# One planner for the output projection and the memory attention: the second half of a transformer layer issued by the list of streams that already issues its first half

## The chip, the cores and the metric

The kernel runs on one core of a Trainium2 chip. A core has TensorE (PE, matrix products into PSUM), VectorE (DVE), ScalarE (ACT), GpSimd (POOL) and SyncE (SP), which here issues all transfers. Each engine takes its instructions strictly in the order in which the program gives them, and waits at an instruction until the semaphores it names have been raised; the engines run beside one another. The metric is the time of one execution on the device in microseconds, as the median of several runs. The kernel before took 1528.05 us (1527.91 to 1530.81 in 3 runs).

## What is computed

One layer of an encoder on 1024 tokens of 1024 features, all in float32. Of the reference, cut to what matters here:

```
h = rmsnorm(x, g_mix_pre);  proj = h @ w_in
y_fox = forgetting_attention(...)            # 8 heads, causal
y_chk = chunked_relpos_attention(...)        # 8 heads, banded
y = concat(rmsnorm(y_fox, g_fox_out), rmsnorm(y_chk, g_chk_out))
x = x + rmsnorm(y @ w_out, g_mix_post)       # output projection
h = rmsnorm(x, g_mem_pre); mem_n = rmsnorm(mem, g_mem_kv)
q = h @ w_mq; k = mem_n @ w_mk; v = mem_n @ w_mv      # 4 heads of 256, 256 memory tokens
y = softmax(q k^T / 16) v @ w_mo
x = x + rmsnorm(y, g_mem_post)
h = rmsnorm(x, g_ff_pre)
x = x + rmsnorm(square(relu(h @ w_ff1)) @ w_ff2, g_ff_post)
```

## The kernel before

**Arithmetic.** Each float32 operand is split in two parts of the type float32r, high (a copy by ACT) and low (the difference, by DVE or POOL). A product is three matmuls, high by high, high by low and low by high (`mm3`, L189 to L193). A weight block of 128 x 1024 is loaded into one of three buffers `wraw`, split by ACT into `whi` and by DVE into `wlo` (two buffers each), and used.

**Tokens.** The tokens are worked in two halves of 512, `th` 0 and 1, and in rows of 128 (`b`). Output features are in two halves `nh`. PSUM has eight banks in four pairs, `mm`, `s`, `tr` and `pv`; a pair is what lets PE write one bank while the other is read.

**The planner.** The attention of both head groups is issued by a small planner that runs while the program is built: class `Flow` (L56). Work is written as streams, generators whose steps each have a cost in PE time and a condition; `Flow.run` (L106) takes, again and again, the first stream in the list whose next step is ready, and what PE's steps bring for the other engines goes to lists with a due time (`put`, L70; `upto`, L86). `Tokens` (L39) count free buffers, `seen` holds when a result is there. `Stock` (L351) holds one list of weight blocks that it loads and splits as buffers come free (`pump`, L401). In the kernel before, its list ends with the memory's key and value weights, `w_mk` and `w_mv`; `memory_steps` (L824), the last filler of the attention phase (L874), makes memory keys `km` and values `vm` with them. All of `w_mk` and `w_mv` has its low part made by DVE, in two halves.

**After attention.** What follows is plain code (L951 to L1150), whose order within each engine a general scheduler of the language decides when the program is built:

- `head_outputs` (L957) loads the stored head outputs of one token half and one group `g` back (`oin`), makes the parts of `yT` and the sums of squares `sq`; `head_rstd` (L981) turns them into a factor for each row by a small matmul `ssh`.
- `mix_out` (L1000) is the output projection, PE tile `yw`: eight blocks of 12 matmuls for each (th, g). With g = 0 ACT evicts a block into `yw` (L1022), with g = 1 DVE adds it (L1024), ACT takes the sum of squares (L992) and DVE multiplies by the gain (L1026). `w_out` is loaded in 12 blocks: those of g = 0 serve both halves, those of g = 1 are loaded for each half.
- `close_block` (L1046) ends four rows: two small POOL operations for a reciprocal root (L200, L201), the residual add (L1053), a store of the row, a sum of squares, a root again, and the normalised row (L1058). `turn` (L1060) transposes the rows on PE (`tr_h`) into `h2T` or `h3T` (L229, L230).
- `cross` (L1064) is the memory attention of one token half: for each head two query blocks `mq`, parts `qh`, `ql` (L1076, L1077), scores `ms`, softmax, transposes `mtr`, and the context product `mo`, into `oT`.
- `mem_out` (L1030) is the output product with `w_mo`, PE tile `ym`. For the second half of tokens `nh` 0 comes from `mem_out`, and `nh` 1 from a list written out by hand from L1363 on, which also issues the last row norms, the transposes `trx` and the first products of the feed-forward part. That hand-written part follows without a planner until the end of the kernel.

Of the kernel before, what the change touches and what calls it, by code (L numbers as in the profile page):

```python
# [55 lines left out]
class Flow:  # L56
# [77 lines left out]
def build(ctx, tc, nc, out, t):  # L134
# [182 lines left out]
    def values(g, w, vs, kb):  # L317
# [8 lines left out]
        if g == 0:  # L326
# [8 lines left out]
            dict(s=2, tr=2, pv=2, mm=2, sp=1, p=2, klo=4, bias=2, raw=2, w=0, u4=6).items()}  # L335
# [15 lines left out]
    class Stock:  # L351
# [3 lines left out]
        def __init__(self):  # L355
            self.blocks = []
            for n, (kind, pr) in enumerate(ORDER):
# [4 lines left out]
                if n > 3:  # L362
                    self.blocks.append((("v", n), t["w_v"][n - 4], [P, KC, P]))
                self.blocks.append((("k", n), t["w_qk"][b + 4], [P, KC, P]))
            self.blocks.append("mem")
            self.blocks += [(("mk", nb), t["w_mk"][nb], [P, KC, P]) for nb in range(KC)]
            self.blocks += [(("mv", nh, kp), row_pair(t["w_mv"], kp, nh), [P, 2, HT])
                            for nh in range(2) for kp in range(4)]
            self.raw, self.w, self.turned = {}, {}, 0
# [10 lines left out]
        def hi(self, key):  # L380
            raw, nm = self.raw[key], "_".join(map(str, key))
            w = [wp.tile(list(raw.shape), F32R, tag=x, bufs=2, name=x + nm) for x in ("whi", "wlo")]
# [3 lines left out]
        def lo(self, key, eng, half):  # L386
            raw, (hi, lo) = self.raw[key], self.w[key]
            n = raw.shape[1] // 2
# [3 lines left out]
        def split_now(self, n):  # L392
# [6 lines left out]
            seen.update({("raw", key): 0.0 for key in self.to_split})  # L399

        def pump(self):  # L401
# [16 lines left out]
            while self.to_split and free["w"].ready() and there(("raw", self.to_split[0])):  # L418
                free["w"].take()
                key = self.to_split.pop(0)  # L420
                vec = key[0] in ("mk", "mv")
                self.turned += 1

                def halves(at, key=key, eng="V" if vec else "G"):
                    cost = 0.61 if eng == "V" else 1.3
                    e = nc.vector if eng == "V" else nc.gpsimd
                    last = lambda end: (seen.__setitem__(key, end), free["raw"].give(end))
                    flow.put(eng, at, cost, lambda: self.lo(key, e, 0), lambda end: flow.put(
                        eng, end, cost, lambda: self.lo(key, e, 1), last, 2), 2)
# [82 lines left out]
    def score_steps():  # L512
        for n, a in heads:
# [57 lines left out]
            for what, m in (("u4", 2), ("klo", 1)):  # L571
                for _ in range(m):
                    free[what].give(flow.end)

# [51 lines left out]
    def value_steps():  # L626
        for n, a, g in units:
# [23 lines left out]
            def leave(pv=pv, nm=f"{n}{a}{g}", own=own, oth=oth, kcol=kcol, g=g, step=1 if kind == "f" else -1):  # L651
# [6 lines left out]
                        ot[own].rearrange("p a b -> p (a b)"))))))  # L658
# [7 lines left out]
    def all_of(key, m):  # L666
# [3 lines left out]
        def one(at):  # L670
            count[0] -= 1
            count[1] = max(count[1], at)
            if count[0] == 0:
                seen[key] = count[1]
        return one
# [148 lines left out]
    def memory_steps(keep):  # L824
        km = Act("km", NM)
        for nb in range(KC):
            for kc in range(0, KC, 2):
                yield 0.72, lambda: kc and there(("mT", kc)) or there(("mk", nb), ("mT", 0)) and free["mm"].ready()
# [7 lines left out]
            free["w"].give(flow.end)  # L836
# [3 lines left out]
        vh = [u4(f"vm_hi{m}", (P, D)) for m in range(2)]  # L840
        vl = [u4(f"vm_lo{m}", (P, D)) for m in range(2)]
        for nh, bank in enumerate(("mm", "s")):
            cs = slice(nh * HT, (nh + 1) * HT)
            ps = []
            for kp in range(4):
                for m in range(2):
                    yield 1.362, lambda: there(("mv", nh, kp)) and (kp or m or free[bank].ready(2))
# [8 lines left out]
                    if kp == 3:  # L856
                        flow.put("S", flow.end, 0.6, lambda m=m, p=ps[m], cs=cs: nc.scalar.activation(vh[m][:, cs], p, AF.Copy),
                                 lambda at, m=m, p=ps[m], cs=cs: flow.put("V", at, 0.7, lambda: nc.vector.tensor_sub(
                                     vl[m][:, cs], p, f(vh[m][:, cs])), free[bank].give, 1), 1)
                free["w"].give(flow.end)  # L860
        keep += [km, vh, vl]

# [11 lines left out]
    def attention_phase():  # L874
# [6 lines left out]
        flow.pumps += [stock.pump, biases.pump]  # L881
        flow.run([value_steps(), turn_steps(), score_steps(), side_steps(), filler_steps(keep)])
        return keep

    flip = [0]
    quiet = [False]

    def lo_eng():
        flip[0] ^= 1
        return nc.vector if flip[0] or quiet[0] else nc.gpsimd  # L890

    def row_pair(w, kp, nh):
        return w[kp * 2 * P:(kp + 1) * 2 * P, nh * HT:(nh + 1) * HT].rearrange(
            "(a p) n -> p a n", p=P)
# [56 lines left out]
    quiet[0] = True  # L951
# [4 lines left out]

    def head_outputs(th, g):  # L957

        yh = [u4(f"yT_hi{th}{g}{i}", (P, 2, HT)) for i in range(2)]
        yl = [u4(f"yT_lo{th}{g}{i}", (P, 2, HT)) for i in range(2)]  # L960
        sq = u4(f"sq{th}{g}", (P, HT), F32)
        for i in range(2):
            o = u4(f"oin{th}{g}{i}", (P, 2, HT), F32)
            for j in range(2):
                kc = g * 4 + i * 2 + j
                nc.sync.dma_start(o[:, j, :], od[kc][th])
                gc = gcol[:, kc:kc + 1]
                dh = yh[i][:, j, :]
                nc.scalar.activation(dh, o[:, j, :], AF.Copy, scale=gc)
                nc.vector.scalar_tensor_tensor(yl[i][:, j, :], o[:, j, :], gc, f(dh),  # L970
                                               op0=ALU.mult, op1=ALU.subtract)
            if i == 0:
                nc.scalar.activation(sq, o[:, 0, :], AF.Square)
                nc.scalar.activation(o[:, 1, :], o[:, 1, :], AF.Square)
            else:
# [832 lines left out]
```

## Time and profile before

| what | value |
|---|---|
| median of 3 runs | 1528.05 us |
| the profiled execution | 1528.19 us |
| its span, first to last instruction | 1526.4 us |
| granted TensorE clock, mean | 0.995 |
| busy: PE, DVE, ACT, POOL | 98%, 62%, 52%, 23% of the span |

The span is what the profiler sees; 1.8 us of the execution lie around it. Times in the views count from the start of the span. The stretch that the change touches runs from the last heads of attention (from about 470 us) to the first transposes of the feed-forward part (`trx`, first at 900.4 us). A matmul's record lasts longer than the distance from its start to the next one's, since matmuls are pipelined; so a PE that is "busy" all the time is not always at its full rate, and the granted clock and the distance between starts have to be read beside it. In the views of waits a line reads: who waited, for whom, total us, times, longest us. In the view of stages each row gives a stretch and its length, then the busy time and the count for PE, PE's weight loads, DVE, ACT and POOL, then the granted clock, the mean share of the 16 transfer engines and GB/s.

### The profile page before, as it was taken

How to read it: one execution, taken by the hardware profiler on the slowest of the kernel's cores; microseconds unless marked ns; L12 is line 12 of the kernel's file. 1: busy time of each engine (PE TensorE's matmuls, PEld its weight loads, DVE VectorE, ACT ScalarE, POOL GpSimd, SP SyncE). 2: the span in 40 equal slices, each digit the busy share in tenths (PEclk: the TensorE clock that was granted, in tenths of full speed). 3: DMA queues.
4: the chain of work that ended last, by engine and by line, in shares of the span. 5: the costliest groups of instructions: out<-in, count | busy, mean ns of one | idle time of the engine just before them, and what ended most of it. 6: DMA issues, size and time to landing. Idle time of an engine off the chain costs nothing. (4 is left out here: it accounts for less than half of the span.)

```text
span 1526.4 us, 21650 instructions
## 1 busy us (share of the span) xinstructions
PE 1492.2 (98%) x7692; PEld 1258.5 (82%) x7692; DVE 945.1 (62%) x1656; ACT 793.1 (52%) x1405; POOL 358.3 (23%) x558
## 2 busy tenths in 40 slices
PE   8999999999999999989999999999999999999998
PEld 7989888788888977778888787888888878888886
DVE  6477676565566755875465477665555575746577
ACT  5367676565566656444344445554555543444442
POOL 4244343343242200221020321433233000000021
PEclk9999999999999999999999999999999999999999
DMA  4222221413123453551252155674445595435575
GB/s 167 88 82 79 80 69 63 147 53 85 38 79 107 143 197 125 178 194 56 70 185 64 43 206 198 223 265 156 152 152 177 199 368 195 150 125 196 190 248 193
DMA packets 83854, 220.68 MB, mean 145 GB/s; under 512 B 9865, under 2 KB 13969, under 8 KB 83746
## 3 DMA queue, kind: packets, MB, share of 16 engines
q1 hardware_dynamic: 83746, 219.30, 43.2%
q8 instruction: 61, 1.00, 0.3%
q14 instruction: 47, 0.39, 0.1%
HBM read 159.96 MB, written 50.91 MB: 138 GB/s over the span
## 5 line engine op out<-in xcount | busy, mean ns | idle before, releaser
L617 DVE TENSOR_TENSOR pl<-ptr,ph 128x512 fp32r<-128x512 f32 (+1 forms) x152 | 91.7, 616 | 43.8 <-ACT ph L620 35.8
L620 ACT ACTIVATE ph<-ptr 128x512 fp32r<-128x512 f32 (+1 forms) x152 | 78.9, 540 | 56.4 <-PE ptr L611 51.1
L1534 ACT ACTIVATE whif<-ra 128x1024 fp32r<-128x1024 f32 x37 | 39.2, 1060 | 121.2 <-PE fy L192 62.6
L1536 DVE TENSOR_TENSOR wlof<-ra,whif 128x1024 fp32r<-128x1024 f32 x37 | 45.3, 1224 | 91.5 <-ACT whif L1534 91.5
L1650 POOL TENSOR_SCALAR rf<-sf 128x1 f32<-128x1 f32 x8 | 8.2, 1027 | 326.9 <-ACT jf L1635 326.6
L186 DVE TENSOR_TENSOR wlo<-wraw,whi 128x1024 fp32r<-128x1024 f32 x44 | 53.6, 1222 | 48.6 <-ACT whi L185 48.3
L647 PE MATMUL pv<-ph,vs 128*128 128x256 f32 x304 | 80.0, 287 | 0.0
L648 PE MATMUL pv<-pl,vs 128*128 128x256 f32 x304 | 78.8, 283 | 0.3 <-DVE pl L617 0.3
L185 ACT ACTIVATE whi<-wraw 128x1024 fp32r<-128x1024 f32 x44 | 46.3, 1058 | 50.0 <-PE ym L193 19.0
L192 PE MATMUL fx<-vlof,whif 128*128 128x512 f32 x168 | 65.5, 390 | 0.0
L193 PE MATMUL fx<-vhif,wlof 128*128 128x512 f32 x168 | 65.4, 389 | 0.0
L191 PE MATMUL fx<-vhif,whif 128*128 128x512 f32 x168 | 65.4, 389 | 0.0
L648 PEld LDWEIGHTS pv<-pl,vs 128*128 128x128 f32 x304 | 57.6, 189 | 5.1 <-DVE pl L617 0.8
L647 PEld LDWEIGHTS pv<-ph,vs 128*128 128x128 f32 x304 | 57.3, 189 | 3.8
L1424 POOL TENSOR_TENSOR sc<-wf,wf 128x512 f32<-128x512 f32 x14 | 22.1, 1581 | 143.6 <-DMA wf<-in_w_ff 111.7
L191 PE MATMUL yw<-whi,yT_hi 128*128 128x512 f32 x128 | 50.4, 400 | 5.2 <-ACT yw L1022 2.8
L191 PE MATMUL k<-hT_hi,whik 128*128 128x512 f32 x128 | 52.8, 412 | 0.0
L191 PE MATMUL mq<-h2T_hi,whi 128*128 128x512 f32 x128 | 51.7, 405 | 0.8 <-DVE yw L1024 0.8
L192 PE MATMUL ym<-wlo,oT_hi 128*128 128x512 f32 x128 | 50.9, 398 | 1.0 <-DVE wlo L186 1.0
L192 PE MATMUL mq<-h2T_lo,whi 128*128 128x512 f32 x128 | 51.6, 403 | 0.0
L193 PE MATMUL mq<-h2T_hi,wlo 128*128 128x512 f32 x128 | 51.5, 402 | 0.0
L191 PE MATMUL q<-hT_hi,whiq 128*128 128x512 f32 x128 | 50.8, 397 | 0.0
(605 smaller groups left out, 5026.2 us busy)
## 6 DMA issues: line engine op xcount, KB each, us to landing
ra<-gd SPq DMA_DIRECT2D x56, 512.0 KB, 3.9
wg<-in_w_ff SPq DMA_DIRECT2D x56, 512.0 KB, 5.2
wf<-in_w_ff SPq DMA_DIRECT2D x38, 512.0 KB, 3.8
gd<-s SPq DMA_DIRECT2D x48, 256.0 KB, 2.1
wraw<-in_w_mq SPq DMA_DIRECT2D x16, 512.0 KB, 4.4
wraw<-in_w_mo SPq DMA_DIRECT2D x16, 512.0 KB, 3.8
gd<-u SPq DMA_DIRECT2D x32, 256.0 KB, 2.1
gd<-g SPq DMA_DIRECT2D x25, 256.0 KB, 2.4
```

The costliest lines, as they stand in the source:

```text
L185: nc.scalar.activation(hi, raw, AF.Copy)
L186: (lo_on or nc.gpsimd).tensor_sub(lo, raw, f(hi))
L191: nc.tensor.matmul(ps, lh, rh, start=start, stop=False, skip_group_check=more)
L192: nc.tensor.matmul(ps, lh, rl, start=False, stop=False, skip_group_check=more)
L193: nc.tensor.matmul(ps, ll, rh, start=False, stop=stop, skip_group_check=more)
L617: flow.put("V", at, 0.7, lambda: nc.vector.tensor_sub(pl[:, live, :], tr[:, live, :], f(ph[:, live, :])), done)
L620: flow.put("S", flow.end, 0.6, lambda ph=ph, tr=tr, live=live: nc.scalar.activation(ph[:, live, :], tr[:, live, :], AF.Copy), split)
L647: nc.tensor.matmul(pv, v, ph[:, hs, :], start=c == 0 and half == 0, stop=False)
L648: nc.tensor.matmul(pv, v, pl[:, hs, :], start=False, stop=c + 1 == len(steps) and half == 1)
L1424: eng.tensor_sub(sc[:, k1], r0[:, k0], r1[:, k0])
L1534: nc.scalar.activation(ah, ra, AF.Copy)
L1536: nc.vector.tensor_sub(al, ra, f(ah))
```

## The change

The plain code between the attention and the hand-written list is replaced by streams of the same planner. `Flow.run` is called a second time, with the list

```
[memory_out_steps(), memory_turn_steps(), memory_score_steps(), rstd_steps(1), second_rows(), second_filler()]
```

so that, whenever its condition holds, a context product, a transpose of probabilities, a score or a transpose of rows is issued, and otherwise the next step of the filler, which is: output projection for g = 0 and for g = 1, queries of half 0, product with `w_mo` of half 0, queries of half 1, and the product of half 1 for `nh` 0. Of the rest:

- All weight blocks, `w_out`, `w_mq` and `w_mo` too, are in the one list of `Stock`. `w_out` is loaded in 8 blocks, and the projection with g = 1 no longer loads its blocks twice. A block's parts live in one of three homes: the `whi`/`wlo` pair, a further pair `wq`, or the general tiles `u4`. DVE makes a low part in one pass instead of two halves; four of the eight `w_mk` blocks have theirs made by POOL in two halves.
- Within the projection the order of the loops changes: one token half is done for both `nh` before the other.
- `Outputs` loads the head outputs of g = 0 as soon as the last scores are issued, in the attention phase; `rstd_steps(0)` is one of the streams there. Its last squares are taken in passes of 512 instead of 1024.
- `Rows` loads the residual rows, two at a time; `close_row` replaces `close_block` by a chain for each row, which begins when its last block is evicted. The two halves of a sum of squares are now added by the POOL operation that adds the constant, and 12 small DVE reductions fall away.
- The loads of the memory tokens stand one place earlier in the list of weights, before the last key block of attention.
- The last four `w_mo` blocks (half 1, `nh` 1) are loaded and split by `Stock` instead of after `mem_out`. The hand-written list itself is not changed.

The diff, cut to its core:

```diff
-    def run(self, streams):
+    def run(self, streams, more=lambda: False):
...
-        while any(h[1] for h in heads):
+        while any(h[1] for h in heads) or more():
...
+        last = self.now
         self.upto(math.inf)
+        self.now = last
...
+            self.blocks += [(("wo", g, nh, i), row_pair(t["w_out"], 2 * g + i, nh), pair)
+                            for g in range(2) for nh in range(2) for i in range(2)]
+            for th in range(2):
+                self.blocks += [(("mq", th, h, nb), t["w_mq"][h * 2 + nb], [P, KC, P])
+                                for h in range(4) for nb in range(2)]
+                self.blocks += [(("mo", th, nh, kp), row_pair(t["w_mo"], kp, nh), pair)
+                                for nh in range(2) for kp in range(4)]
+            self.home = {("wo", 0, 1, 0): "wq", ("wo", 0, 1, 1): "u4", ("wo", 1, 1, 0): "wq", ("wo", 1, 1, 1): "u4"}
+            self.home.update({("mk", nb): "u4" for nb in range(1, KC, 2)})
+            self.home.update({("mv", nh, kp): "u4" for nh in range(2) for kp in (1, 3)})
...
-                vec = key[0] in ("mk", "mv")
+                vec = key[0] not in "qkv" and (key[0] != "mk" or key[1] % 2)
...
+    def mix_steps(g):
+        for th, nh in ((0, 0), (0, 1), (1, 0), (1, 1)):
+            cs = slice(nh * HT, (nh + 1) * HT)
+            for b in range(4):
+                c = slice(b * P, (b + 1) * P)
+                for k in range(4):
+                    yield (0.681, lambda: k % 2 or there(("wo", g, nh, k // 2)) and (k or
+                           there(("y", th, g), ("rs", th, g)) and free["mm"].ready()
+                           and (("w", th) in ys or free["u4"].ready(4))))
...
+    def second_filler():
+        yield from mix_steps(0)
+        yield from mix_steps(1)
+        yield from query_steps(0)
+        yield from product_steps(0, (0, 1))
+        yield from query_steps(1)
+        yield from product_steps(1, (0,))
...
-        flow.run([value_steps(), turn_steps(), score_steps(), side_steps(), filler_steps(keep)])
+        flow.pumps += [stock.pump, biases.pump, outputs.pump]
+        flow.run([value_steps(), turn_steps(), score_steps(), side_steps(), rstd_steps(0),
+                  filler_steps(keep)])
...
-    mix_out((0,), 1)
-    mixed(0)
-    mix_out((1,), 1, after={1: turn_mixed(0)})
-    mixed(1)
...
-    o = cross(1, h2[1], after={0: lambda: turn(y0, 0, h3[0], "h3")})
+    with tc.manual_schedule():
+        free["wq"].give(flow.now)
+        for key, src in (("mix", "g_mix_post"), ("mem", "g_mem_pre")):
+            gains[key] = gain(p2, t[src], src)
+        flow.pumps[1] = Rows().pump
+        flow.run([memory_out_steps(), memory_turn_steps(), memory_score_steps(), rstd_steps(1), second_rows(),
+                  second_filler()], lambda: stock.to_load or stock.to_split)
...
-    mem_out(1, o, y, ss, gmpost, (0,))
-    wo = [load_w(row_pair(t["w_mo"], kp, 1), [P, 2, HT], u4, lo_eng()) for kp in range(4)]
+    wo = [stock.w["mo", 1, 1, kp] for kp in range(4)]
```

More of the change, by code (lines that the diff above doesn't have):

```diff
@@ L399, in split_now, with done @@
             seen.update({("raw", key): 0.0 for key in self.to_split})
+        def done(self, key):
+            home = self.home.get(key, "w")
+            for _ in range(1 + (home == "u4")):
+                free[home].give(flow.end)
         def pump(self):
@@ L626, in value_steps @@
     def value_steps():
+        landed = [all_of(("od", k), 32) for k in range(2)]
         for n, a, g in units:
@@ new lines, in build, with rstd_steps, add, root @@
+    outputs = Outputs()
+    def rstd_steps(g):
+        for th in range(2):
+            yield 0.5, lambda: there(("sq", th, g)) and free["pv"].ready()
+            free["pv"].take()
+            sq = parts[th, g][2]
+            rs = parts["rs", th, g] = small.tile([P, 4], F32, tag="rs4", bufs=4, name=f"rs{th}{g}")
+            ps = mm_tile([P, 4], f"ssh{th}{g}", "pv")
+            for b in range(4):
+                nc.tensor.matmul(ps[:, b:b + 1], sq[:, b * P:(b + 1) * P], o512, start=True, stop=True)
+            free["u4"].give(flow.end)
+            def add(rs=rs, ps=ps):
+                nc.vector.tensor_scalar(rs, ps, EPS, None, op0=ALU.add)
+            def root(at, rs=rs, key=("rs", th, g)):
+                free["pv"].give(at)
+                flow.put("G", at, 1.1, lambda: nc.gpsimd.tensor_tensor(rs, rs, mhalf[:, 0:4], op=ALU.pow), mark(key))
+            flow.put("V", flow.end, 0.16, add, root)
@@ L955, in build @@
     p2x = pool("p2x", stack=p2xs)
[L957 to L975, printed above, removed]
-                nc.scalar.activation(o, o, AF.Square)
-                nc.vector.tensor_add(sq, sq, o[:, 0, :])
-            nc.vector.tensor_add(sq, sq, o[:, 1, :])
-        return yh, yl, sq
```

549 lines of the change are left out of this document (362 added, 187 removed).

## The prediction

> **What bounds the kernel now.** I read the page first: the span, the shares of the engines and the chain that ended last.
>
> ```profile
> span 1526.4 us, 21650 instructions
> PE 1492.2 (98%) x7692; PEld 1258.5 (82%) x7692; DVE 945.1 (62%) x1656; ACT 793.1 (52%) x1405; POOL 358.3 (23%) x558
> PE 38%; DVE 1%; ACT 0%; DMA 0%; issue 0%; DVEq 0%; POOLq 0%; SPq 0%; POOL 0%; ACTq 0%
> ```
>
> TensorE (PE) is the bound and everything else runs beside it. The built programs hold 7740 matmuls each, in the same shapes, so the change can only move the time in which PE stands still or runs slowly. The next view cuts the changed stretch (515 to 885 us) by stages; columns are PE, weight loads, DVE, ACT, POOL, granted clock, DMA share and GB/s.
>
> ```profile
> 515.00:548.00 33.00, 31.57 (x171) 26.55 (x170) 21.07 (x36) 18.15 (x28) 1.77 (x7) 1.00 0.77 255
> 548.00:600.00 52.00, 48.69 (x222) 38.89 (x220) 23.25 (x34) 30.45 (x45) 3.06 (x3) 1.00 0.33 105
> 600.00:650.00 50.00, 47.57 (x216) 38.24 (x216) 38.42 (x50) 22.76 (x43) 9.87 (x17) 1.00 0.56 179
> 650.00:680.00 30.00, 25.37 (x106) 19.78 (x105) 21.99 (x32) 14.76 (x31) 8.24 (x16) 0.89 0.57 193
> 680.00:780.00 100.00, 100.00 (x511) 84.50 (x511) 48.94 (x85) 41.91 (x88) 8.43 (x18) 1.00 0.25 80
> 780.00:870.00 90.00, 90.00 (x473) 76.48 (x472) 50.05 (x85) 41.55 (x84) 23.20 (x37) 1.00 0.33 106
> 870.00:885.00 15.00, 12.84 (x48) 9.64 (x47) 8.39 (x9) 8.19 (x14) 2.17 (x2) 0.89 0.36 129
> 919.00:937.00 18.00, 14.77 (x70) 11.43 (x68) 16.10 (x25) 10.10 (x17) 0.00 (x0) 1.00 0.31 108
> 1250.00:1300.00 50.00, 50.00 (x222) 41.39 (x221) 25.18 (x23) 20.14 (x22) 0.00 (x0) 1.00 0.62 219
> ```
>
> PE idles 1.43 + 3.31 + 2.43 + 4.63 + 2.16 = 13.96 us between 515 and 885; the cross attention itself (680 to 870) has no idle at all. The view of waits, cut to 535 to 885, names what it waits for:
>
> ```profile
> PE yw L191 <- ACT yw L1022: 2.8, 3, 1.3
> PE ms L193 <- DVE ql L1077: 2.4, 1, 2.4
> PE yw L191 <- DVE yw L1024: 2.4, 3, 1.1
> PE mv L192 <- DVE wlomv L390: 1.3, 2, 1.1
> PE tr_h L216 <- DVE h2T_lo L230: 1.1, 2, 0.7
> PE ym L191 <- ACT whi L185: 1.1, 1, 1.1
> PE ym L192 <- DVE wlo L186: 1.0, 2, 0.8
> PE mq L191 <- DVE yw L1024: 0.8, 1, 0.8
> ```
>
> Each is PE standing at the head of its fixed order for an eviction, a row norm or a weight split while other matmuls could have run. The longest, and what follows it, in order of time:
>
> ```profile
> 667.81 0.28 PE L192 MATMUL ms<-km_lo,qh 128*128 128x256 f32 x1
> 670.51 0.39 PE L193 MATMUL ms<-km_hi,ql 128*128 128x256 f32 x1 [2.42 <-DVE ql L1077]
> ...
> 671.34 0.40 PE L191 MATMUL mq<-h2T_hi,whi 128*128 128x512 f32 x1
> 671.57 0.41 PE L192 MATMUL mq<-h2T_lo,whi 128*128 128x512 f32 x1
> ...
> 672.20 0.63 PE L191 MATMUL mq<-h2T_hi,whi 128*128 128x512 f32 x1
> 672.63 0.63 PE L192 MATMUL mq<-h2T_lo,whi 128*128 128x512 f32 x1
> ```
>
> A matmul of 512 columns starts 0.23 us after the one before (50 / 222 in the dense window); after the stall it takes 0.43, and so for some 3 us. The granted clock of 0.89 in two windows says what this costs: 0.11 x 30 + 0.11 x 15 = 4.95 us. A record lasts 0.39 where starts lie 0.23 apart, so each of the 15 waits listed also loses about 0.16 us of overlap that idle time does not show: 2.4 us. What can be removed is therefore 13.96 + 4.95 + 2.4 = 21.3 us.
>
> [...]
>
> **The change, part by part.** Prices come from these groups (548 to 700 us for DVE and ACT, 590 to 660 for the root on POOL; the attention phase for the two of L390; then landing times).
>
> ```profile
> L186 DVE TENSOR_TENSOR wlo<-wraw,whi 128x1024 fp32r<-128x1024 f32 x19 | 23.1, 1221 | 19.1 <-ACT whi L185 19.1
> L1024 DVE SCALAR_TENSOR_TENSOR yw<-yw,rs,yw 128x512 f32<-128x512 f32 x16 | 11.7, 743 | 1.1 <-PE yw L193 1.1
> L1026 DVE TENSOR_TENSOR yw<-yw,g_mix_post 128x512 f32<-128x512 f32 x16 | 10.7, 685 | 0.6 <-ACT junk L992 0.4
> L1053 DVE SCALAR_TENSOR_TENSOR xth<-yw,h2y,xth 128x1024 f32<-128x1024 f32 x8 | 10.2, 1281 | 2.8 <-POOL h2y L201 2.8
> L1058 DVE SCALAR_TENSOR_TENSOR yw<-xth,h2x,g_mem_pre 128x1024 f32<-128x1024 f32 x8 | 10.2, 1280 | 4.1 <-POOL h2x L201 4.1
> L970 DVE SCALAR_TENSOR_TENSOR yT_lo<-oin,gcol,yT_hi 128x512 fp32r<-128x512 f32 x12 | 8.6, 747 | 6.9 <-ACT yT_hi L969 6.8
> L230 DVE TENSOR_TENSOR h2T_lo<-tr_h,h2T_hi 128x512 fp32r<-128x512 f32 x8 | 5.4, 684 | 2.1 <-ACT h2T_hi L229 2.1
> L992 ACT ACTIVATE junk<-yw 128x512 bf16<-128x512 f32 x16 | 10.0, 628 | 8.1 <-DVE yw L1024 7.8
> L201 POOL TENSOR_TENSOR h2y<-h2y,mhalf 128x1 f32<-128x1 f32 x5 | 3.2, 635 | 0.4
> L185 ACT ACTIVATE whi<-wraw 128x1024 fp32r<-128x1024 f32 x18 | 18.8, 1057 | 15.7 <-PE mq L192 6.2 <-DMA wraw<-in_w_out 5.1 <-PE yw L192 2.3
> L390 DVE TENSOR_TENSOR wlomk<-wrawmk,whimk 128x512 fp32r<-128x512 f32 x11 | 8.0, 747 | 0.0
> L390 POOL TENSOR_TENSOR wlok<-wrawk,whik 128x512 fp32r<-128x512 f32 x12 | 15.3, 1295 | 7.4 <-ACT whik L383 7.3
> wraw<-in_w_out SPq DMA_DIRECT2D x12, 512.0 KB, 4.9
> oin<-od SPq DMA_DIRECT2D x16, 256.0 KB, 4.6
> ```
>
> *Weights in one list.* w_out is loaded in 8 blocks instead of 12: four transfers, four ACT copies (4 x 1.06) and four DVE subtractions (4 x 1.22) go, all beside PE, so 0 us. The last four w_mo blocks are split inside the streams, ahead of the second token half's last product; the 2.16 us idle and the slow clock of 870 to 885 (1.65) end. Its first half keeps only two split buffers; block 2 may be split after product step 6 and is used at step 9, with two context products between: 4 x 1.36 = 5.4 us of PE against 1.06 + 1.22 = 2.3, covered.
>
> *Evictions and row norms as streams.* The output product now runs one token half after the other. The four rows of the first half close while PE has the other half's eight blocks (8 x 12 x 0.225 = 21.6 us); the second half's rows close under the first half's queries (64 x 3 x 0.225 = 43 us). A row needs 0.74 (sum), 0.63 (square), 0.69 (gain), two passes of 0.64 for the root, 1.28 (add), 1.06 (square, as ACT's other pass of that width), the root again and 1.28: 8.2 us of chain. With two buffers for x the rows go in pairs, a load of 4 to 5 us between: some 20 us. Both are covered, so the waits for L1024, L230 and L1077 go.
>
> *Where DVE runs out.* Between the first block with g = 1 and the first query matmul the built order gives DVE 16 x 0.743 + 14 x 0.685 + 8 x 1.28 + 3 x 1.22 + 4 x 0.747 + 5 x 0.684, and three sums for 2.1: 43.9 us. PE has there 15 blocks (40.5) and 28 transposes and a row-sum, for which I put 4, an estimate (28 x 128 columns are 7 matmuls of 512, 1.6 us, and small ones run below that rate): 44.5 us. DVE also stands in order for POOL's roots (2.8 and 4.1 us over eight rows above, so 3.5 for the four here): 47.4. Between 0 (its waits fall where PE is ahead) and 6 us (twice the excess of 2.9) I take 2, near the excess.
>
> *A weight block out of turn.* In the built order ACT copies block (nh 0, pair 1) of w_out behind the two blocks of nh 1, although PE needs it after only two matmul groups. The raw of the second of them waits for a buffer that (nh 0, pair 0) gives back, and that one's raw for the buffer of block kp 1 in the last half of w_mv. From the low part of that block: 4.9 + 1.06 + 1.22 + 4.9 + 1.06 + 1.06 + 1.22 = 15.4 us. PE needs the result three blocks (3 x 2.7) and half an output block (1.35) after it starts on kp 1: 9.5 us. If kp 1 is split just in time, as the 1.3 us wait for wlomv above says it is now, PE stands 5.9 us; if it is split a landing time and more ahead, 0. I take the middle, 2.9.
>
> *Head outputs inside the last heads.* Eight transfers, sixteen ACT passes and fourteen DVE ones (8 x 0.747 and 6 sums near 0.69, 10 us) move from 530 to 560 into the tail of attention and the memory values, where DVE already has 21.07 of 33 us. Sums wait on oin (4.6 us); on PE the row-sum stands in front of the values. Between -1.4 (all idle of 515 to 548 goes) and +4 (a second wait as long as a load) I take +1.
>
> *Key weights on POOL.* Four of eight w_mk blocks move their low part to POOL: DVE -4 x 1.49, and the other four as one pass -4 x 0.27, POOL +8 x 1.295. The softmax scale on POOL stands behind one half, 1.3 us; PE has a w_mk block (5.4 us) to run meanwhile. 0, with ends -1 and +4.
>
> *SP's queue.* In the built order two gain rows and two x rows stand ahead of the last w_mv block and all of w_out. They wait for attention's buffers. The last w_mv block is used 19 us later than the first, against four transfers of about 5 that overlap; 0, counted within the term above.
>
> *Unchanged.* From the first transposes of the feed-forward part the DVE order is the same; the 3.23 us of idle at 919 to 937 stay.
>
> Sum: -21.3 + 2 + 2.9 + 1 = -15.4. The profiled execution took 1528.19 us (1526.4 span, 1.8 around it), 0.14 above the median of 1528.05. Prediction 1528.2 - 15.4 = **1512.8 us**.
>
> **The rivals.**
> - *Half of it.* The streams' order was fixed ahead, and each DVE or ACT queue stands where a transfer is late. The bad ends above are 6 + 5.9 + 4 + 4 = 19.9; with somewhat over half of them, 11, it is 1528.2 - 21.3 + 11 = 1518, with nearly all 1526. For it: all of w_out and of the head outputs come through one queue with two or three buffers. Against: behind each joint after the first, matmuls of another stream stand ready.
> - *More.* None of the three new stalls comes, 1528.2 - 21.3 = 1507, and DVE's relief of 4 x 1.49 + 4 x 0.27 = 7 us in the tail of attention reaches PE in part, 5: 1502. For it: DVE is what mv waits for there. Against: these stalls are also short now.
> - *Slower.* DVE becomes the bound while rows close. Then each output block (two PSUM buffers) starts with a stall of about 1 us, and the clock stays at half for 12 matmuls: 1 + 0.16 + 12 x 0.2 = 3.6 us a block. It decides from the fifth of 16 blocks (5 x 3.6 = 18, above the 15.4 gained); with eight it is 1512.8 + 29 = 1542. For it: 47.4 against 44.5. Against: the 1.3 us stalls at 548 to 600 kept a clock of 1.00.
> - *No effect.* The same waits come back at other joints: 1528.
>
> **How the numbers follow.** Forecast (1507 to 1517) 0.52; half (1517 to 1525) 0.18; more (below 1507) 0.14; no effect 0.06; slower 0.10. A measurement of this kernel tells a change from none at about 0.2%, 3 us. Faster 0.84, same 0.06, slower 0.10. The range 1501 to 1523 leaves out the slower case, no effect and the outer ends of half.
>
> **What would show it.** PE idle in the stretch from the memory values to the feed-forward's first transposes falls from 14 us to about 6; the granted clock there is 1.00 in all 30 us stretches; no wait of ms for ql; one wait of yw for a part of w_out near its start, about 3 us; waits of yw for its eviction while rows close, 2 us together. Wrong would be a clock under 0.9 in the output product, DVE above 95% there, or ACT standing for oin with yw behind it.

## The result

The changed kernel takes 1508.12 us (median of 4 runs, 1506.40 to 1509.48), the kernel before beside it 1528.67 us (4 runs, 1527.91 to 1530.81): a ratio of 0.9863, 95% interval 0.9846 to 0.9880, a gain of 20.5 us. Forecast were 1512.8 us, 1501 to 1523. The profiled execution of the changed kernel took 1506.4 us, 21.8 less than that of before; it is the fastest of the four. One later execution of the changed kernel, 2482.85 us at a granted clock of 0.557, was slow as a whole and stands in no median below.

The page of the changed kernel: span, engines, and the chain that ended last.

```profile
span 1504.6 us, 21583 instructions
PE 1481.1 (98%) x7692; PEld 1255.8 (83%) x7692; DVE 937.4 (62%) x1620; ACT 791.1 (53%) x1405; POOL 385.7 (26%) x566
PE 75%; DVE 3%; ACT 1%; issue 1%; POOL 1%; DMA 1%; SPq 0%; DVEq 0%; POOLq 0%; ACTq 0%
```

PE's records are as many as before; 67 instructions of all engines are gone, and POOL has 27 us more. The shares alone would not tell that anything happened. The stages do; columns are stretch, length, PE, weight loads, DVE, ACT, POOL, granted clock, DMA share, GB/s. The cuts follow the work, which ends earlier now.

```profile
515.00:548.50 33.50, 30.86 (x168) 26.25 (x168) 24.81 (x35) 22.50 (x37) 4.40 (x8) 1.00 0.68 223
548.50:600.00 51.50, 51.20 (x230) 42.19 (x229) 15.19 (x19) 23.58 (x37) 1.93 (x1) 1.00 0.32 102
600.00:650.00 50.00, 48.83 (x236) 40.62 (x235) 44.84 (x60) 27.52 (x59) 20.41 (x27) 1.00 0.40 137
650.00:680.00 30.00, 30.00 (x171) 25.77 (x170) 24.44 (x37) 17.71 (x37) 6.74 (x11) 1.00 0.63 218
760.00:780.00 20.00, 18.52 (x95) 15.24 (x94) 16.53 (x20) 12.06 (x23) 9.89 (x13) 1.00 0.65 231
780.00:865.00 85.00, 84.94 (x437) 71.87 (x437) 47.04 (x76) 38.94 (x79) 21.20 (x26) 1.00 0.26 82
898.00:916.00 18.00, 15.73 (x75) 12.31 (x74) 16.10 (x24) 10.43 (x17) 0.00 (x0) 1.00 0.32 104
```

Two of the stages had a granted clock of 0.89 before; now all have 1.00. PE's idle between 515 and 865 is 2.64 + 0.30 + 1.17 + 1.48 + 0.06 and 0.05 in the stage left out, 5.7 us, against 13.96. Of the 5.7, 2.6 lie in the tail of attention, ahead of the memory values, where the kernel before had no idle; 3.1 lie behind. What is left of waits, 470 to 930 us (who waits, for whom, total us, times, longest):

```profile
PE pv L694 <- DVE pl L662: 2.6, 4, 1.6
PE tr_h3T L1135 <- DVE ym L1057: 1.5, 1, 1.5
PE tr_h2T L1135 <- DVE h2T_lo L1142: 1.2, 1, 1.2
PE px L193 <- ACT whi_a L1458: 1.1, 1, 1.1
PE px L195 <- DVE wlo_a L1461: 1.1, 2, 0.6
PE yw L194 <- DVE wlowo L418: 0.3, 1, 0.3
```

The waits of `yw`, `ms`, `mv`, `mq` and `ym` for an eviction or a split that were there before are gone but for 0.3 us. How much the stretch gained is read from two marks, the first matmul of the memory values and the first transpose of the feed-forward part (shapes, count, duration in ns, first and last start). Before:

```profile
L191 PE MATMUL mv<-whimv,mT_hi x32: 387/389/494, 524.2 to 547.6; 128*128 128x512 f32 x32
L1294 PE MATMUL trx<-ident,ym x32: 270/272/273, 900.4 to 927.5; 128*128 128x128 f32 x32
```

After:

```profile
L193 PE MATMUL mv<-whimv,mT_hi x32: 387/389/486, 525.0 to 548.0; 128*128 128x512 f32 x32
L1542 PE MATMUL trx<-ident,ym x32: 270/272/273, 879.8 to 906.0; 128*128 128x128 f32 x32
```

Both traces hold the same 1728 matmul records from mark to mark. The stretch was 376.2 us and is 354.8: 21.4 us of the 21.8. Attention, which now carries the head outputs, ends 0.8 us later; behind `trx` 1.2 us are saved (626.0 to 624.8), most of it a shorter wait of `px` in the hand-written list.

### The profile page after: what moved, and what is told of

Same layout as the page of the kernel before. It is cut to its first block, busy times and chain, and to the rows that moved or that the text cites. A ratio compares the mean times of both kernels' runs of the same rounds, so it can differ in the third digit from the quotient of the medians.

```text
span 1504.6 us, 21583 instructions
## 1 busy us (share of the span) xinstructions
PE 1481.1 (98%) x7692; PEld 1255.8 (83%) x7692; DVE 937.4 (62%) x1620; ACT 791.1 (53%) x1405; POOL 385.7 (26%) x566
## 4 chain that ended last, share of the span: by engine, by line
PE 75%; DVE 3%; ACT 1%; issue 1%; POOL 1%; DMA 1%; SPq 0%; DVEq 0%; POOLq 0%; ACTq 0%
PE fx L194 4%; PE fx L195 4%; PE fx L193 4%; PE fy L193 3%; PE fy L194 3%; PE fy L195 3%; PE px L195 3%; PE px L194 3%; PE px L193 3%; PE ptr L656 2%; PE yw L194 2%; PE yw L195 2%; PE yw L193 2%; PE pz L195 2%; PE pz L194 2%; PE pz L193 2%
## 5 line engine op out<-in xcount | busy, mean ns | idle before, releaser
L193 PE MATMUL mq<-h2T_hi,whimq 128*128 128x512 f32 x128 | 52.1, 407 | 0.0
L193 PE MATMUL ym<-whimo,oT_hi 128*128 128x512 f32 x128 | 50.3, 394 | 0.1
L193 PE MATMUL yw<-whiwo,yT_hi 128*128 128x512 f32 x128 | 50.3, 393 | 0.0
L194 PE MATMUL yw<-wlowo,yT_hi 128*128 128x512 f32 x128 | 49.9, 390 | 0.3 <-DVE wlowo L418 0.3
L195 PE MATMUL k<-hT_hi,wlok 128*128 128x512 f32 x128 | 50.2, 392 | 0.0
L195 PE MATMUL q<-hT_hi,wloq 128*128 128x512 f32 x128 | 50.1, 392 | 0.0
L195 PE MATMUL mq<-h2T_hi,wlomq 128*128 128x512 f32 x128 | 50.1, 391 | 0.0
```

The costliest lines, as they stand in the source:

```text
L193: nc.tensor.matmul(ps, lh, rh, start=start, stop=False, skip_group_check=more)
L194: nc.tensor.matmul(ps, lh, rl, start=False, stop=False, skip_group_check=more)
L195: nc.tensor.matmul(ps, ll, rh, start=False, stop=stop, skip_group_check=more)
```

## The experiments

The theory (A): the gain is that PE has another stream's matmul to issue where its fixed order made it stand, and that the clock then stays at full rate. The rivals: (B) it is the work that was taken away (four weight blocks, twelve small DVE passes, key weights on POOL); (C) it is the weight list alone. The rivals of single steps are told with them. Times are medians, compared with the changed kernel's 1508.1. The ratio to the kernel before is given with each.

**One sequence in place of streams.** The same instructions, weight list and buffers; the steps come head after head in one stream.

```diff
+        for th in range(2):
+            for h in range(4):
+                yield from take(q[th], 16)
+                yield from take(s, 4)
+                yield from take(t_, 2)
...
+                yield from take(o_, 2)
...
-        flow.run([memory_out_steps(), memory_turn_steps(), memory_score_steps(), rstd_steps(1), second_rows(),
-                  second_filler()], lambda: stock.to_load or stock.to_split)
+        flow.run([rstd_steps(1), one_stream()], lambda: stock.to_load or stock.to_split)
```

> The steps of the output product, the rows and the memory attention are issued in one fixed sequence (head after head: queries, scores, turns, outputs), with the weight list, buffers, evictions and number of instructions of the changed kernel. Theory (the gain comes from having other matmuls to issue while an eviction, a softmax or a row norm is under way): TensorE stands once or twice a head for the chain score, maximum, exponent, scale, turn, eviction (about 2.5 + 1.8 us), eight heads, with the half rate behind each stall (1.6 to 3 us): 50 to 80 us longer than the changed kernel's 1508, so 1558 to 1588, and the granted clock below 0.95 in the stretch of the memory attention. Rival (less work: four weight blocks fewer, twelve small passes fewer, key weights on POOL): within 3 us of 1508.

Measured: 1576.5 us, ratio 1.0316 (1.0299 to 1.0333), 68 us more than the changed kernel. Its waits, 470 to 960 us, and two stages of the memory attention:

```profile
PE ms L193 <- ACT mp L1194: 10.7, 9, 2.1
PE mtr L1219 <- POOL mp L1197: 8.3, 14, 1.4
PE tr_h2T L1135 <- DVE h2T_lo L1142: 4.5, 5, 2.4
PE mo L193 <- ACT ph L1222: 4.1, 6, 0.7
```

```profile
650.00:750.00 100.00, 85.28 (x393) 66.65 (x391) 47.28 (x79) 38.22 (x78) 11.32 (x22) 0.91 0.26 90
800.00:900.00 100.00, 81.33 (x375) 63.17 (x374) 44.94 (x76) 35.92 (x75) 16.38 (x27) 0.93 0.23 74
```

The links of the softmax's chain appear one by one as waits, and the granted clock is 0.91 and 0.93 in these stages. Under B or C alone this kernel should have kept 1508; with all of that work gone and the list in place it is slower than the kernel before. It is a harder order than that one's, so the 68 us are no measure of the change's gain. The next experiment changes less.

**Rows with less cover.** The blocks of the output product with g = 1 in the order of before.

```diff
-        for th, nh in ((0, 0), (0, 1), (1, 0), (1, 1)):
+        for th, nh in ((0, 0), (0, 1), (1, 0), (1, 1)) if g == 0 else ((0, 0), (1, 0), (0, 1), (1, 1)):
```

> The second half (g = 1) of the output product goes through its blocks as in the kernel before, both token halves for the first 512 columns and then both for the second, so that the rows of the first token half close with only four blocks (10.9 us) of other matmuls left in place of eight (21.7 us). Theory: a chain of about 20 us in pairs of rows is then uncovered by about 9 us, and the half rate adds up to 3: 8 to 12 us longer than the changed kernel, 1516 to 1520, with TensorE idle between the output product and the first memory queries waiting for DVE or POOL. Rival (the order of the blocks does not matter, DVE's 44 us of work there set the time): within 3 us of 1508.

Measured: 1525.3 us, ratio 0.9979 (0.9969 to 0.9988): 17 us more, most of the gain. Waits, then the stages:

```profile
PE tr_h2T L1135 <- DVE yw L1057: 8.1, 2, 5.2
PE ssh L989 <- DVE sq L951: 3.8, 1, 3.8
```

```profile
600.00:650.00 50.00, 43.31 (x192) 35.59 (x190) 35.75 (x49) 22.05 (x49) 14.96 (x22) 0.93 0.25 85
650.00:700.00 50.00, 44.20 (x232) 37.45 (x233) 35.50 (x52) 24.48 (x48) 11.28 (x18) 0.90 0.53 190
```

The 8.1 us are the expected 9: a chain of some 20 us less 10.9 us of cover. DVE is less busy here than in the changed kernel (35.75 against 44.84 of 50), so it is the latency of the chain and not DVE's amount of work. Two things were not foreseen: the row sum `ssh` of the other token half is needed four blocks earlier and waits 3.8 us, and the half rate (granted clock 0.93 and 0.90 in the two stages) takes the rest, 17 - 11.9 + 1.2 (the wait it replaces) = 6 us. Work and weight list are the changed kernel's, so neither B nor C alone can be the cause: with them in place, most of the gain goes when these blocks change their order.

**Four weight blocks twice again.** `w_out` of g = 1 is loaded and split for each token half.

```diff
-                            for g in range(2) for nh in range(2) for i in range(2)]
+                            for g in range(3) for nh in range(2) for i in range(2)]
...
-            if th == 1:
+            if th == 1 or g:
                 for k in range(2):
-                    stock.done(("wo", g, nh, k))
+                    stock.done(("wo", g + (g and th), nh, k))
```

> The four blocks of w_out with g = 1 are loaded and split once for each token half again: 12 loads, 12 copies on ACT (4 x 1.06 us more) and 12 subtractions on DVE (4 x 1.22 more), as many as in the kernel before. Theory (that work lay beside TensorE): 0 to +1.5 us against the changed kernel, 1508 to 1510. Rival (the gain is work taken away): up to 4 x 2.28 = 9 us come back, 1517. A third reading: DVE is at 90% while rows close (44.8 of 50 us), so 4.9 us more there push it past TensorE, +3 to +5 us, with waits for DVE between 620 and 660.

Measured: 1515.8 us, ratio 0.9915 (0.9900 to 0.9930), 7.7 us more. A wait and a stage:

```profile
PE tr_h2T L1136 <- DVE yw L1058: 4.1, 2, 2.1
```

```profile
600.00:650.00 50.00, 45.28 (x209) 37.19 (x208) 47.08 (x62) 29.24 (x59) 22.49 (x25) 0.95 0.51 173
```

The theory's 0 to 1.5 us is wrong here. The time lies within rival B (up to 9) and above the third reading (3 to 5); the place speaks for the third. DVE has 47.08 of 50 us, the rows close later, the transposes wait 4.1 us in place of 1.2, and the half rate makes up the rest (granted clock 0.95 in this stage, 0.98 from 650 to 700 and 0.97 from 900 to 950 us: 0.05 x 50 + 0.02 x 50 + 0.03 x 50 = 5.0 us); no load and no copy is waited for. DVE is at its limit in this stage, as the prediction's 43.9 (or 47.4 with POOL) against 44.5 us said. As many passes more on DVE, put where it is not at its limit, cost nothing (the key weights below).

**The last `w_mo` blocks late.** Loaded and split after the streams, as before.

```diff
-                                for nh in range(2) for kp in range(4)]
+                                for nh in range(2 - th) for kp in range(4)]
...
-    wo = [stock.w["mo", 1, 1, kp] for kp in range(4)]
+    wo = [load_w(row_pair(t["w_mo"], kp, 1), [P, 2, HT], u4, nc.vector) for kp in range(4)]
```

> The last four blocks of w_mo are loaded and split after the streams have ended, as in the kernel before, and not from the weight list; all else is the changed kernel's. Theory: the idle of 2.16 us and the slow clock of 870 to 885 (0.11 x 15 = 1.65 us) that the kernel before had at this place come back: +3.8 us, 1512, with a wait of ym for these blocks and a granted clock under 0.95 around it. Rival (the stall there belonged to the fixed order of the product, not to the late blocks): 0, 1508.

Measured: 1513.3 us, ratio 0.9903 (0.9888 to 0.9918), 5.2 us more (expected 3.8):

```profile
PE ym L193 <- ACT whi L187: 1.1, 1, 1.1
PE ym L194 <- DVE wlo L188: 1.0, 2, 0.8
PE px L195 <- DVE wlo_a L1461: 2.2, 2, 1.7
```

The two waits of `ym` that stood in the profile of before are back, with a stretch at half rate behind them (granted clock 0.97 from 850 to 900 us), and a wait further on in the hand-written list is longer (2.2 against 1.1). This part of the gain is the list's: C holds for it, but for these 4 to 5 us alone. The prices of single steps (17, 7.7 and 5.2 us) come to more than the whole gain of 20.5; each says what is lost when that step alone is undone, and they are no shares of it. Of B, the twelve small DVE passes were not tried by themselves.

**Head outputs later.** They start after the last transposes of attention, not after the last scores.

```diff
+        seen["turned"] = flow.end
...
-                if not (there(("od", g), "scored") and free["u4"].ready(7) and (g == 0 or ("w", 1) in ys)):
+                if not (there(("od", g), "turned") and free["u4"].ready(7) and (g == 0 or ("w", 1) in ys)):
```

> The head outputs are loaded and scaled only after the last transposes of attention's probabilities, not already after the last scores. In the changed kernel TensorE stands 3.5 us there (518 to 524 us, four waits of pv for pl), where DVE has yT_lo, wlomv and an addition that waits 0.77 us for a store ahead of pl. Theory (head outputs crowd DVE in attention's tail): the waits of pv fall from 3.5 to about 1.5 us, the output product starts no later because the memory values (24 us) cover loads and scaling: 1506. Rival (the waits belong to the chain pl, pv itself): the waits stay, and the first yw may come up to 4 us later: 1508 to 1512.

Measured: 1513.2 us, ratio 0.9900 (0.9885 to 0.9914), 5 us more:

```profile
PE ssh L990 <- DVE sq L952: 2.3, 1, 2.3
PE yw L193 <- ACT whiwo L412: 1.5, 1, 1.5
PE yw L194 <- DVE wlowo L418: 0.5, 1, 0.5
PE pv L695 <- DVE pl L662: 0.3, 1, 0.3
```

Both were right in half: the waits of `pv` go (2.6 to 0.3), as the theory had it, and the memory values and the output product pay more for it, as the rival had it: 4.3 us in the other three waits, and three stretches of 3.4 us at half rate behind them, 4.8 us (granted clock 0.66 from 542 to 547 us and 0.57 from 552 to 560). Against this later start, the early start of the head outputs is a good trade.

**Key weights on DVE.** POOL's share of the `w_mk` low parts goes back to DVE.

```diff
-                vec = key[0] not in "qkv" and (key[0] != "mk" or key[1] % 2)
+                vec = key[0] not in "qkv"
```

> All low parts of the memory key weights on DVE, none on POOL: DVE +4 x 1.22 us between 470 and 525. By the prediction's term for this part: 0, with ends -4 and +1, 1504 to 1509. By the rival of a larger gain (DVE's relief in attention's tail reaches TensorE): up to +5 us, 1513, with longer waits of pv for pl or of mv for wlomv.

Measured: 1507.6 us, ratio 0.9863 (0.9848 to 0.9878): no change. The waits of `pv` for `pl` stay about as they were (2.4 us in four). That part of the change is worth nothing by itself, as the prediction had it.

**An honest cost for the root.** The planner counts 0.95 us for a root on POOL.

```diff
-                    ("G", 0.95, lambda: root(1, s2)),
+                    ("G", 1.5, lambda: root(1, s2)),
...
-        flow.put("G", at, 0.95, lambda: root(0, ss[:, 0:1], ss[:, 1:2]), wait, 1)
+        flow.put("G", at, 1.5, lambda: root(0, ss[:, 0:1], ss[:, 1:2]), wait, 1)
```

> The order is worked out with 1.5 us for a root on POOL in place of 0.95; instructions are the same. The changed kernel's two stalls behind row norms (transposes of h2 1.33 us, of h3 1.64 us) end in theory (the order was fixed on a row that closes earlier than it does): -1.5 to -3 us, 1505 to 1506.5. Rival (DVE and POOL cannot be faster there, the stall moves to the next step): 1508.

Why it was tried stands in the order of time of the changed kernel; PE has begun a group of transposes of two rows, and the second row waits for a root that took 1.31 + 0.57 us:

```profile
766.51 1.31 POOL L1008 TENSOR_SCALAR rm<-s2m 128x1 f32<-128x1 f32 x1
767.91 0.57 POOL L1011 TENSOR_TENSOR rm<-rm,mhalf 128x1 f32<-128x1 f32 x1
...
768.51 1.28 DVE L1057 SCALAR_TENSOR_TENSOR ym<-xtm,rm,g_ff_pre 128x1024 f32<-128x1024 f32 x1 [0.76 <-POOL rm L1011]
...
769.85 0.87 PE L1135 MATMUL tr_h3T<-ident,ym 128*128 128x128 f32 x6 [1.48 <-DVE ym L1057]
```

Measured: 1506.3 us, ratio 0.9857 (0.9838 to 0.9876), not to be told from the changed kernel. The wait of `tr_h3T` is gone; that of `tr_h2T` grew from 1.2 to 2.0, and in the profiled execution one stretch at half rate came behind `pv` (granted clock 0.97 from 500 to 550 us). Theory and rival each had one of the two places.

**Pauses of known length.** 20 pauses in the dense last product, to see what a stall costs beyond itself.

```diff
+        def pause(s, widths):
+            a, b = ops[s - 1][1], ops[s][3]
+            for w in widths:
+                nc.vector.tensor_sub(a[:, D - w:], f(a[:, D - w:]), f(a[:, D - w:]))
+            nc.vector.tensor_sub(b[:, 0:1], f(b[:, 0:1]), f(a[:, D - 1:]))
```

> The changed kernel with 20 pauses for TensorE in the dense last product, 10.8 us apart: each second step waits for a chain of DVE subtractions on tiles of the step before, in five lengths (about 0.9, 1.3, 1.8, 2.5 and 3.1 us), four times each. The first changes no value that the product uses (a low part is already used up, then zero is subtracted from one column). First reading (length alone decides, between the 1.87 us that kept the rate and the 2.42 us that did not): the 12 short pauses keep starts 0.23 us apart, the 8 long ones are followed by 8 to 10 starts of 0.43. Second (idle counts as a share of windows that run on their own): pauses of 1.3 to 2.5 us halve the rate in some places and not in others. [...] Time: 1508 + 4 x (0.9 + 1.3 + 1.8 + 2.5 + 3.1) = 1546, and about 1.7 for each halving: 1546, 1560 and between.

Measured: 1548.35 us in one run. By the distance from start to start, less the usual 0.23, the pauses were 0.65, 0.91, 1.45, 2.17 and 2.71 us, four of each, 31.6 us together. None of the three short lengths is followed by slow starts; all four of 2.17 are; of the longest, 2.71, only one of four is. The granted clock says the same: 0.97 in five of the six stages of 50 us from 1200 us on, one stretch at half rate in each. In order of time, a pause of 2.17 and one of 2.71:

```profile
1292.61 0.39 PE L193 MATMUL fx<-bh,ah 128*128 128x512 f32 x1
1295.01 0.72 PE L194 MATMUL fx<-bl,ah 128*128 128x512 f32 x1 [2.01 <-DVE bl L1945]
1295.52 0.63 PE L195 MATMUL fx<-bh,al 128*128 128x512 f32 x1
1295.95 0.63 PE L193 MATMUL fx<-bh,ah 128*128 128x512 f32 x1
...
1298.08 0.60 PE L195 MATMUL fx<-bh,al 128*128 128x512 f32 x1
1298.51 0.41 PE L193 MATMUL fx<-bh,ah 128*128 128x512 f32 x1
1298.76 0.40 PE L194 MATMUL fx<-bl,ah 128*128 128x512 f32 x1
...
1307.39 0.39 PE L193 MATMUL fx<-vhif,whif 128*128 128x512 f32 x1
1310.33 0.50 PE L194 MATMUL fx<-vlof,whif 128*128 128x512 f32 x1 [2.54 <-DVE vlof L1945]
1310.66 0.39 PE L195 MATMUL fx<-vhif,wlof 128*128 128x512 f32 x1
1310.89 0.40 PE L193 MATMUL fx<-vhif,whif 128*128 128x512 f32 x1
```

After the shorter pause eight starts lie 0.43 apart, and at 1298.5 the full rate returns; after the longer one the rate never falls. Eight starts of 0.427 are 3.4 us, and the trace of the kernel before has the same length: its granted clock is 0.50 in three stretches of 3.41 us between the marks, each shown here behind the 3.41 us ahead of it:

```profile
651.34:654.75 3.41, 1.93 (x10) 1.17 (x9) 3.41 (x8) 3.33 (x11) 0.14 (x1) 1.00 0.30 117
654.75:658.16 3.41, 3.41 (x10) 2.63 (x9) 3.41 (x6) 0.46 (x1) 0.65 (x2) 0.50 0.08 14
668.41:671.82 3.41, 1.31 (x9) 1.22 (x10) 3.41 (x5) 1.48 (x3) 1.69 (x2) 1.00 1.01 303
671.82:675.23 3.41, 3.41 (x10) 2.63 (x9) 2.64 (x4) 0.00 (x0) 1.95 (x3) 0.50 0.91 315
873.21:876.62 3.41, 1.51 (x7) 0.69 (x5) 2.26 (x3) 2.97 (x6) 0.00 (x0) 1.00 0.00 0
876.62:880.03 3.41, 3.41 (x8) 2.73 (x9) 2.36 (x2) 1.13 (x2) 0.00 (x0) 0.50 0.55 167
```

They begin 17.07 and 204.80 us apart, which is 5 and 60 times 3.413. So the second reading fits: idle counted in windows that run on their own, here of 3.41 us. If windows of the run with pauses end at 1298.5 and every 3.41 us before and after, the one from 1291.7 to 1295.1 holds the whole of the 2.17 us, while the longer pause (1307.6 to 1310.3) is cut at 1308.7 into 1.1 and 1.6. The other two that cost nothing are cut the same way, the largest piece 1.72 us; the one that did cost left 2.2 us in one window. Here a window with 2.17 us of idle was followed by one at half rate, and one with 1.72 was not. A halving cost 8 x 0.2 = 1.6 us, and the time fits: 1508.1 + 31.6 + 5 x 1.6 = 1547.7. This run is one execution, but the same count holds in all 13 traces together (distances from start to start, in windows set by the changes of the granted clock, 30 to 1490 us): all 26 windows at full rate that lost more than 2.0 us were followed by the half rate, and of the 100 that lost 0.9 to 2.0 only three. The kernel before has three of the first kind (2.03, 2.21 and 2.34 us, those above) and nine of the second (0.94 to 1.57), the changed kernel none and seven (0.95 to 1.90); of these sixteen none was followed by it.

**The changed kernel again, and two versions meant to be better.** The first is the changed kernel without an edit. The second gives attention's output tiles a third buffer; the third adds the root's cost of 1.5.

```diff
-                ot = p1.tile([P, 2, P], F32, tag="ot", bufs=2, name=f"ot{nm}")
-                o2 = p1.tile([P, 2, P], F32, tag="o2", bufs=2, name=f"o2{nm}")
+                ot = p1.tile([P, 2, P], F32, tag="ot", bufs=3, name=f"ot{nm}")
+                o2 = p1.tile([P, 2, P], F32, tag="o2", bufs=1, name=f"o2{nm}")
```

> The changed kernel itself, beside the two that follow. Expected 1508 (1506 to 1510). The phase of the clock's windows is not the program's to choose, so its stalls of 1.3 to 1.9 us should cost a half rate stretch (about 1.7 us) in some executions and not in others.

> Attention's output tiles get three buffers in place of two, the scratch tile beside them one in place of two. Theory (in attention's tail DVE stands 0.77 us for the store of an output tile and pl queues behind it): the waits of pv fall from 3.5 to about 2.5 us, -1 us: 1507. Rival (one scratch buffer makes ACT wait through the whole of attention): slower, 1509 to 1515.

> Both the buffers of the run before and the cost of 1.5 us for a root on POOL in the planner: no wait of the transposes of h3 (-1.64), shorter waits of pv (-1): 1505 to 1506. Rival: the order of the rows' other steps gets worse with it, as the transposes of h2 did (1.33 to 2.13 us): 1507 to 1508.

Measured: the changed kernel again 1508.2 us (three executions), ratio 0.9861 (0.9845 to 0.9878); with three output buffers 1506.9, 0.9860 (0.9844 to 0.9876); with both 1504.95, 0.9847 (0.9833 to 0.9860). The last is the fastest seen, some 3 us below the changed kernel, at the edge of what these intervals can tell. Its waits:

```profile
PE tr_h2T L1135 <- DVE h2T_lo L1142: 2.0, 1, 2.0
PE pv L694 <- DVE pl L662: 1.9, 4, 0.9
```

`pv` waits 1.9 us in place of 2.6 and at most 0.9 at a time, and `tr_h3T` not at all. The second profile of the changed kernel has the same waits as the first to 0.2 us, and yet:

```profile
core 0: 1507.9 us, clock 0.996
```

Two stretches at half rate, from 524 and from 916 us, behind `pv` and `px` (granted clock 0.97 from 500 to 550 and from 900 to 950 us), make the 3.3 us of difference between two executions of one program (2 x 1.6). So the spread of its runs is in part, by the reading above, where the windows of 3.41 us cut its stalls, and a change of 1 or 2 us in a stall can't be read from two executions.

## Why the prediction was right

The forecast of 1512.8 lay 4.7 us above the median and 6.4 above the profiled execution. By its steps, from the profiles:

- *What can be removed, 21.3 us.* Right in place; too small. From mark to mark 21.4 us went, and the changed kernel's stretch holds three stalls that the one before had not (0.46, 1.33 and 1.64 us by distances from start to start, 3.4 together). So 24.8 went. Of the three terms two hold: the idle, 13.96, lies wholly between the marks, and the half rate, forecast at 4.95, measured 4.8 (three stretches of eight starts, each 0.2 late). The term that was too small is "0.16 us of overlap" for each of 15 waits, 2.4: it measured 6.1. By distances, 23 starts came over 0.15 us late, not 15; beyond the idle that the profile shows, they lost 4.2 us, and the start behind each was late as well (0.34 us in place of 0.23), 1.9 together. A busy share does not show this.
- *Weights in one list, 0 us; the last blocks 2.16 + 1.65.* Right for the last blocks (5.2 by experiment against 3.8). The four blocks that went were priced at nothing, and that is wrong for the new order: put back into it they cost 7.7 us. The cover was named, PE, but four of the passes fall where DVE was known to be short; the two parts of the prediction were not put together.
- *Where DVE runs out, 2 us.* One stall of 1.33, by the named cause, in the named stage. The second, `tr_h3T` with 1.64, was not foreseen: the rows of the memory attention's output also close through POOL's roots, and PE's order was fixed on 0.95 us for what took up to 1.9.
- *A block out of turn, 2.9 us.* It measured 0.46. The chain was right: from the low part of the block of `w_mv` (533.75 + 1.22) to the end of that of `w_out` (549.48 + 1.23) it is 15.7 us, 15.4 predicted. The start was a guess, the middle between just in time and a landing ahead; in fact the `w_mv` block was split some 5 us ahead of its use, and PE asked for the block of `w_out` 15.3 us later, at 550.30.
- *Head outputs inside the last heads, 1 us.* Near in size: attention ends 0.8 us later. That is a balance: 2.6 us of new waits of `pv` in its last microseconds, against, among others, idle that went earlier in attention (0.9 us from 470 to 515). Against a later start it is worth 5 us.
- *Key weights on POOL, 0 us.* Right, by experiment. *Hand-written list, unchanged:* its wait became about 1 us shorter.
- *Slower, as a rival.* Its mechanism, DVE short while rows close and the half rate behind stalls, showed when four passes more were put in (DVE at 47.08 of 50 us, granted clock 0.95, 7.7 us). No run shows the 12 matmuls at half rate of its price: a stretch at half rate held 8 starts of 512 columns, 0.427 us apart, and the half rate did not follow each stall. The changed kernel stands just on the near side of it.
- *What would show it.* Idle 14 to about 6, from the memory values on: 3.1, and 2.6 more ahead of them. Clock 1.00 in all stages: yes, in the first profile. No wait of `ms` for `ql`: none. One wait of `yw` for a part of `w_out`, about 3 us: 0.3. Waits of `yw` for its eviction, 2 us: none; it was the transposes that waited, 1.2 us.

Against the profiled execution, two errors went the same way and were small: 3.5 us too little removed and some 2 us too much added, beside the 1.2 us behind `trx`. That the added part came so near is in part luck: a stall that I did not foresee (`tr_h3T`) took the place of those that did not come.

## What to carry to other kernels

Where one engine is the bound, a list of streams is worth the stalls of its fixed order, and the stages with idle and a lower granted clock say how much; take the time between two marks of the bound engine rather than its busy share, since late starts behind a stall hide in "busy" (6.1 us in the kernel before). Then ask of each helper engine in which stage it is near its limit: work taken from it is worth nothing elsewhere (key weights: 0) and much there (four passes: 7.7 us). When an order is fixed while building, a cost that is too low for a step moves a stall; correct it and look where the next one comes up.

## What the runs showed of the hardware

The half rate of the clock did not follow from a stall's length alone. A pause of 2.71 us cost nothing more in three of four places, one of 2.17 cost 1.6 us in all four, and the pair of waits of `px`, 1.32 and 0.70 us within 3.4 us, was followed by the half rate in one execution of the changed kernel and not in the other. None of the 12 pauses of 0.65 to 1.45 us was followed by it.

Some of POOL's small operations took up to 2.6 times as long as others of their kind while DVE was busy. The second step of a root on 128 x 1 (two of its groups in the kernel before: 0.64 and 0.57 us on average from 590 to 660 us) took in the changed kernel, from 600 to 650 us, with DVE at 90%:

```profile
L1011 POOL TENSOR_TENSOR rw<-rw,mhalf 128x1 f32<-128x1 f32 x13 | 9.6, 737 | 1.1
```

Ten of these 13 took 0.56 to 0.58 us, as in the kernel before, and three 0.96 to 1.5. From 600 to 650 us the share of such steps over 0.7 us went with DVE's work: 1 of 10 with DVE at 72% (rows with less cover), 1 of 8 at 77% (the kernel before), 3 of 13 at 90%, and 6 of 12 at 94% (four weight blocks twice). Over all traces but that of the pauses, DVE was at work 95% of the time of the 110 slow steps and 50% of that of the 370 quick ones (in the changed kernel alone 95% for 9 and 50% for 31, in the kernel before 89% for 7 and 40% for 33). Spans on POOL are rough; why some steps are quick beside a busy DVE stays open.
